# Hybrid decoder layer on one core: the first norm's factor moved into the activations, and four projections fed high and low activations at once

## The chip, the cores and the metric

The kernel runs on one core of a Trainium2 chip. The metric is the device time of one execution in microseconds. TensorE multiplies, VectorE (DVE) and ScalarE (ACT) work elementwise, GpSimd (POOL) too, and SyncE (SP) issues DMAs.

## The reference, cut to what matters

One layer: an RMSNorm of the input, one combined projection whose columns feed three token mixers (HGRN2, Mamba-2, RWKV-7) and the sigmoid gates that merge them, then an output projection, and a squared-ReLU MLP behind a second norm.

```python
u = rmsnorm(h, ln1_w[l])            # x * rsqrt(mean(x*x) + eps) * w
p = u @ w_comb                      # all input projections: q f i g | z xs B C dt | r k v ... | gates
q = silu(q_raw); g = sigmoid(g_raw) # HGRN2
y = y * silu(z)                     # Mamba-2
gates = sigmoid(p_gate)             # 3 branches x 2048
mixed = gates[0]*(o_h @ w_up_h) + gates[1]*(o_m @ w_up_m) + gates[2]*(o_r @ w_up_r)
h = h + mixed @ w_out
u = rmsnorm(h, ln2_w[l])
h = h + square(relu(u @ w_mlp_in)) @ w_mlp_out
out = rmsnorm(h, lnf_w)
```

There are 256 tokens and 16 learned ones before them (272 columns, `T`); the width is 2048, which is 16 blocks of 128 (`KT`).

## The kernel before

Activations lie with channels in the partitions and tokens in the columns. A product makes one tile of 128 output channels: it goes through the 16 blocks of input channels and adds up in one PSUM bank. To keep float32 accuracy every operand is split in a high part, rounded to the type `fp32r`, and a low part, what is left; of the four products of parts three are made. `product` (L229) does that with three matmuls per block: weights high by activations high, weights high by activations low, weights low by activations high. `product2` (L243) does the first two as one matmul of twice the columns (512): the result stands in two halves of the bank, which the caller adds. Before, the output projection and the MLP use `product2`; the input projection and the three branch projections use `product`.

`weights` (L213) loads a tile's weights in pieces of 8 blocks (512 KB, on SP's queue, three raw buffers) and splits each on ScalarE (L201, the cast) and VectorE (L202, the low part); there are three buffers for the high parts and three for the low ones, so about a tile and a half ahead. It runs with high priority.

The input norm (L290 to L367). `x_parts` multiplies x by the norm's weight `ln1` and splits it into `uh` and `ul`, without the norm's factor. The first four column tiles (`FIRST`: wl, aldt and two of gl) run while x and their weights arrive. The squares of x are summed by ScalarE (L359) and GpSimd (L361, L362), a matmul with ones sums over the partitions (L364), and `inv_sqrt` makes the factor `rstd1`, one per token. Since the factor depends on the token alone, it is applied to each result: `proj` (L369) multiplies the PSUM tile by `rstd1` (L371), and L367 does so for the first four. Constants (`omu` to `lbt`, L378 to L397) are worked out behind the last part of x.

After that come the stages of RWKV-7 (`r_stage1`, `r_inverse`, `r_solve`; tiles r, k, v), of Mamba-2 (`m_tile`, `m_gate`; tiles xs, z, B, C), of the gates (`gates_ahead`, written to DRAM until they are needed) and of HGRN2 (`h_cols`, `h_chain`; tiles f, i, q, g), placed among each other by hand; then the branch projections, the output projection, the MLP. PSUM has three banks for such tiles (`trunk_psum`) and five for the rest (`mx`).

The order of instructions on each engine is made by a planner: it plays the program through with estimated times and takes on each engine the instruction of highest priority that is ready; program order is the priority, a `tc.high_priority()` block comes ahead of it, and `tc.issue_after(ins)` sets an instruction behind another one on its engine. On the chip each engine then runs its list in order.

## Time and profile before

| | |
|---|---|
| median of 3 runs | 1914.78 us (1914.56 to 1915.48) |
| the profiled execution | 1914.41 us |
| its span, first to last instruction | 1912.6 us |
| TensorE (PE) busy | 1890.1 us, 99% |
| weight loads (PEld) busy | 1747.1 us, 91% |
| VectorE busy | 1289.5 us, 67% |
| ScalarE busy | 1074.5 us, 56% |
| GpSimd busy | 187.5 us, 10% |
| read from HBM | 327.72 MB (written 10.08 MB; 177 GB/s over the span) |

Busy time of TensorE is modelled: a matmul's row lasts longer than the time until the next one may start, so the time of a stream is read from starts, not from durations. Of a matmul, `pt<-uh,wh` names the output tile and the operands, and `128x256` the partitions and columns of the output. A few matmul records can be missing from a trace.

### The profile page before, as it was taken

The page shows a single profiled execution, that of the slowest core. Times are in us where ns is not written, and L with a number is a line of the kernel's source. Part 1 is how long each engine was busy: PE and PEld are TensorE (multiplying, and loading weights), DVE is VectorE, ACT ScalarE, POOL GpSimd, SP SyncE. Part 2 cuts the span into 40 slices and gives each one's busy share as a digit, 9 for nine tenths or more (in the row PEclk, how much of TensorE's full clock was granted, in tenths as well). Part 3 has the DMA queues.
Part 4 walks back from the last instruction along what each step waited for, and adds up shares of the span by engine and source line. Part 5 has one row for each costly group of instructions (what it writes and reads, how often), then busy time and mean ns, then how long its engine had stood idle before and what let it go on. Part 6 is the DMA issues. An engine that isn't in the chain of part 4 may idle for free.

```text
span 1912.6 us, 35367 instructions
## 1 busy us (share of the span) xinstructions
PE 1890.1 (99%) x13910; PEld 1747.1 (91%) x13910; DVE 1289.5 (67%) x2126; ACT 1074.5 (56%) x1943; POOL 187.5 (10%) x317
## 2 busy tenths in 40 slices
PE   7999999999999999999999999999999999999997
PEld 7999999999999999999999988888888888888886
DVE  7878667567956566777677776654566556675575
ACT  6666566566556667766564455544454345435554
POOL 5110111112111111112111100000000000000000
PEclk9999999999999999999999999999999999999998
DMA  6556544354554445445656765555555555555552
GB/s 241 181 187 198 159 145 154 127 164 157 177 165 155 144 144 194 144 146 169 203 166 212 251 220 193 185 187 188 186 187 187 188 186 187 188 187 188 187 187 100
DMA packets 104103, 340.12 MB, mean 178 GB/s; under 512 B 18216, under 2 KB 21432, under 8 KB 103936
## 3 DMA queue, kind: packets, MB, share of 16 engines
q1 hardware_dynamic: 92480, 316.79, 50.3%
q0 software_dynamic: 8576, 17.67, 3.0%
q10 hardware_dynamic: 2880, 3.39, 0.5%
q8 instruction: 109, 1.79, 0.4%
q14 instruction: 58, 0.48, 0.1%
HBM read 327.72 MB, written 10.08 MB: 177 GB/s over the span
## 4 chain that ended last, share of the span: by engine, by line
PE 98%; DVE 1%; DMA 0%; ACT 0%; issue 0%; SPq 0%; DVEq 0%
PE pt L251 28%; PE pt L239 15%; PE pt L237 15%; PE pt L238 15%; PE pt L253 14%; PE px L1093 1%; PE px L619 1%; DMA xt<-in_xt 0%; PE px L725 0%; PE px L707 0%; PE px L633 0%; PE px L762 0%; PE px L627 0%; PE px L548 0%; PE px L346 0%; PE px L691 0%
## 5 line engine op out<-in xcount | busy, mean ns | idle before, releaser
L202 DVE TENSOR_TENSOR wl<-raw,wh 128x1024 fp32r<-128x1024 f32 (+1 forms) x593 | 726.4, 1225 | 397.3 <-ACT wh L201 389.4
L201 ACT CAST wh<-raw 128x1024 fp32r<-128x1024 f32 (+1 forms) x593 | 621.9, 1049 | 652.8 <-PE pt L238 239.1
L237 PE MATMUL pt<-uh,wh 128*128 128x256 f32 (+2 forms) x1984 | 567.9, 286 | 0.0
L239 PE MATMUL pt<-uh,wl 128*128 128x256 f32 (+3 forms) x1984 | 567.4, 286 | 0.0
L238 PE MATMUL pt<-ul,wh 128*128 128x256 f32 (+2 forms) x1984 | 567.0, 286 | 0.0
L237 PEld LDWEIGHTS pt<-uh,wh 128*128 128x128 f32 x1984 | 374.1, 189 | 3.4 <-issue 1.5
L239 PEld LDWEIGHTS pt<-uh,wl 128*128 128x128 f32 x1984 | 373.9, 189 | 3.4 <-issue 1.9
L238 PEld LDWEIGHTS pt<-ul,wh 128*128 128x128 f32 x1984 | 373.4, 188 | 3.7 <-issue 1.7
L251 PE MATMUL pt<-z,wh 128*128 128x512 f32 x1024 | 362.2, 399 | 0.0
L251 PE MATMUL pt<-hx,wh 128*128 128x512 f32 x1024 | 358.9, 393 | 0.0
L253 PE MATMUL pt<-hx,wl 128*128 128x256 f32 x1024 | 287.9, 283 | 0.0
L253 PE MATMUL pt<-z,wl 128*128 128x256 f32 x1024 | 287.4, 281 | 0.0
L251 PEld LDWEIGHTS pt<-z,wh 128*128 128x128 f32 x1024 | 192.4, 188 | 48.0
L251 PEld LDWEIGHTS pt<-hx,wh 128*128 128x128 f32 x1024 | 191.6, 188 | 43.6
L253 PEld LDWEIGHTS pt<-z,wl 128*128 128x128 f32 x1024 | 193.4, 189 | 0.1
L253 PEld LDWEIGHTS pt<-hx,wl 128*128 128x128 f32 x1024 | 192.5, 188 | 0.9
L239 PE MATMUL pt<-oh,wl 128*128 128x256 f32 x384 | 108.3, 282 | 0.0
L237 PE MATMUL pt<-oh,wh 128*128 128x256 f32 x384 | 108.2, 282 | 0.0
L238 PE MATMUL pt<-ol,wh 128*128 128x256 f32 x384 | 107.3, 279 | 0.0
L371 DVE TENSOR_TENSOR pt<-pt,rstd 128x256 f32<-128x256 f32 (+3 forms) x124 | 54.1, 436 | 56.2 <-PE pt L239 55.7
L251 PE MATMUL pt<-m,wh 128*128 128x512 f32 x256 | 89.8, 393 | 0.0
L1298 POOL TENSOR_TENSOR macc<-h,rs 128x256 f32<-128x256 f32 x3 | 2.1, 720 | 825.9 <-ACT rs L1292 825.9
(459 smaller groups left out, 2218.2 us busy)
## 6 DMA issues: line engine op xcount, KB each, us to landing
raw<-in_w SPq DMA_DIRECT2D x591, 512.0 KB, 3.5
rcb<-sc_rc SPq DMA_DIRECT2D x8, 256.0 KB, 3.7
sc_gr<-gt POOLq DMA_DIRECT2D x16, 128.0 KB, 3.6
sc_gm<-gt POOLq DMA_DIRECT2D x16, 128.0 KB, 3.6
sc_gh<-gt POOLq DMA_DIRECT2D x16, 128.0 KB, 3.6
gin<-sc_gr POOLq DMA_DIRECT2D x16, 128.0 KB, 2.7
gin<-sc_gm POOLq DMA_DIRECT2D x16, 128.0 KB, 2.8
gin<-sc_gh POOLq DMA_DIRECT2D x16, 128.0 KB, 3.3
```

The lines of the kernel that those rows point to most:

```text
L201: act.copy(dst_h, src)
L202: vec.tensor_tensor(dst_l, src, dst_h.bitcast(F32), sub)
L237: pe.matmul(ps, lhsT=wh[:, j], rhs=hi[:, kt, tok], start=(kt == 0), stop=False)
L238: pe.matmul(ps, lhsT=wh[:, j], rhs=lo[:, kt, tok], start=False, stop=False)
L239: pe.matmul(ps, lhsT=wl[:, j], rhs=hi[:, kt, tok], start=False, stop=(k == last and j == 7))
L251: pe.matmul(full.rearrange("p (a n) -> p a n", a=2), lhsT=wh[:, j], rhs=x[:, :, kt], start=(kt == 0), stop=end, skip_group_check=True)
L253: pe.matmul(full[:, :NR], lhsT=wl[:, j], rhs=x[:, 0, kt], start=False, stop=end, skip_group_check=True)
L371: vec.tensor_tensor(ps, ps, rstd1[:, tok], mult)
L619: pe.matmul(pk[e][:, c], lhsT=kt_[er, t], rhs=ar[er, :, t], start=True, stop=True)
L1093: pe.matmul(px[br, 2 * i + c], lhsT=xc, rhs=xc, start=True, stop=True)
L1298: nc.gpsimd.tensor_tensor(macc[:, c], h1[:, c], rf, mult)
```

## The change

The factor moves from the results into the activations. The first four tiles still run on x times `ln1` and get their multiplication afterwards. The rest of the kernel uses other activations: when the factor is there, x is multiplied in place by `ln1` and the factor (16 instructions on VectorE) and split again into `uh` and `ul` (four splits of four blocks each, ScalarE and VectorE), which overwrites what the first four tiles read. `proj` is then only `product`, without a multiplication. The additions of the squares move from GpSimd to VectorE, the last of them becomes a second matmul with ones, and the whole chain gets high priority, except the 16 multiplications. `uh` and `ul` become halves of one tile `u`, so that one access pattern reaches both.

A new helper, `proj2`, makes the tiles of the gates and of z, q and g with `product2` over the 256 real tokens: ScalarE copies the low half out of PSUM, VectorE adds it to the high one. For the gates and g the sum goes to SBUF, for z and q it stays in PSUM. The constants `lbt` of HGRN2 move to the beginning of that stage.

```diff
@@ -283,13 +283,13 @@
     st_u = ExitStack()
     upool = pool(st_u, "upool")
-    uh = upool.tile([P, KT, T], F32R, name="uh")
-    ul = upool.tile([P, KT, T], F32R, name="ul")
-    rstd1 = upool.tile([P, T], F32, name="rstd1")
+    u = upool.tile([P, 2, KT, T], F32R, name="u")
+    uh, ul = u[:, 0], u[:, 1]
     with ExitStack() as st:
         np_ = pool(st, "norm1", side="right")
         xt = np_.tile([P, KT, T], F32, name="xt")
+        rstd1 = np_.tile([P, T], F32, name="rstd1")
         FIRST = (("wl", ALL), ("aldt", ALL), (("gl", 0), REAL2), (("gl", 1), REAL2))
         def raw_piece(key, k, parts=1):
@@ -353,22 +353,34 @@
                     x_parts(4 * i + 4, 4 * i + 8)
         ssum = np_.tile([P, 2, T], F32, name="ssum")
-        for q in range(8):
-            sq = np_.tile([P, 2, T], F32, tag="sq", bufs=2, name=uname("sq"))
-            with tc.issue_after(last_x[0]):
-                act.activation(sq if q else ssum, xt[:, 2 * q:2 * q + 2], AF.Square)
-            if q:
-                nc.gpsimd.tensor_tensor(ssum, ssum, sq, add)
-        nc.gpsimd.tensor_tensor(ssum[:, 0], ssum[:, 0], ssum[:, 1], add)
-        ssq = mx()[:, :T]
-        pe.matmul(ssq, lhsT=C("ones"), rhs=ssum[:, 0], start=True, stop=True)
-        inv_sqrt(rstd1, ssq, 1.0 / D, eps_n)
+        with tc.high_priority():
+            for q in range(8):
+                sq = np_.tile([P, 2, T], F32, tag="sq", bufs=2, name=uname("sq"))
+                with tc.issue_after(last_x[0]):
+                    act.activation(sq if q else ssum, xt[:, 2 * q:2 * q + 2], AF.Square)
+                if q:
+                    with tc.issue_after(last_x[1]):
+                        vec.tensor_tensor(ssum, ssum, sq, add)
+            ssq = mx()[:, :T]
+            for k in range(2):
+                pe.matmul(ssq, lhsT=C("ones"), rhs=ssum[:, k], start=(k == 0), stop=(k == 1))
+            inv_sqrt(rstd1, ssq, 1.0 / D, eps_n)
+        for kt in range(KT):
+            vec.scalar_tensor_tensor(xt[:, kt], xt[:, kt], V("ln1", kt), rstd1, mult, mult)
+        with tc.high_priority():
+            for q in range(4):
+                s = slice(4 * q, 4 * q + 4)
+                split(uh[:, s], ul[:, s], xt[:, s])
         for ps, (_, tok) in zip(first, FIRST):
             vec.tensor_tensor(ps, ps, rstd1[:, tok], mult)
     def proj(key, tok=ALL, ahead=True):
-        ps = product(key, uh, ul, tok, ahead=ahead)
-        vec.tensor_tensor(ps, ps, rstd1[:, tok], mult)
+        return product(key, uh, ul, tok, ahead=ahead)
+
+    def proj2(key, t):
+
+        ps, lo = product2(key, u[:, :, :, NM:])
+        act.copy(t, lo)
         return ps
@@ -384,17 +396,6 @@
     nwa = const.tile([P, 16], F32, name="nwa")
     vec.tensor_scalar(nwa, V("w0", 0, 16), -1.0, None, mult)
     nw0, na0 = nwa[:, 0:8], nwa[:, 8:16]
-
-    lbt = const.tile([P, 6, 8], F32, name="lbt")
-    lg = V("lb", 0, 8)
-    vec.tensor_tensor(lbt[:, 0], lg, lg, ALU.max)
-    vec.tensor_tensor(lbt[:, 1], lg, lbt[:, 0], sub)
-    act.activation(lbt[:, 1], lbt[:, 1], AF.Exp)
-    vec.reciprocal(lbt[:, 2], lbt[:, 1])
-    vec.tensor_tensor(lbt[:, 3], lbt[:, 1], lbt[:, 2], mult)
-    vec.tensor_tensor(lbt[:, 4], lbt[:, 3], lbt[:, 3], sub)
-    vec.tensor_scalar(lbt[:, 5], lbt[:, 4], -1.0, 1.0, mult, add)
-    lb, omlb = lbt[:, 4], lbt[:, 5]
     late.close()
@@ -923,8 +924,9 @@
         vec.scalar_tensor_tensor(o_m[:, t], xs[:, NM:], V("md", t), py[:, :NR], mult, add)
     def m_gate(t):
-        ps = proj(("z", t), REAL)
         s = mt("zs", NR)
+        ps = proj2(("z", t), s)
+        vec.tensor_tensor(ps, ps, s, add)
         sigmoid(s, ps)
         vec.tensor_tensor(s, ps, s, mult)
         vec.tensor_tensor(o_m[:, t], o_m[:, t], s, mult)
@@ -958,9 +960,10 @@
                 return
             key = early[len(sc_g)]
             sc_g[key] = dr.tile([P, NR], F32, name=f"sc_{key[0]}{key[1]}")
-            ps = proj(key, REAL)
             t = wp.tile([P, NR], F32, tag="gt", bufs=2, name=uname("gt"))
-            sigmoid(t, ps)
+            ps = proj2(key, t)
+            vec.tensor_tensor(t, ps, t, add)
+            sigmoid(t, t)
             nc.gpsimd.dma_start(sc_g[key], t)
     m_open()
@@ -1013,6 +1016,18 @@
     def ht(tag, shape, bufs=1):
         return hp.tile([P, *shape], F32, tag=tag, bufs=bufs, name=uname(tag))
+
+    lbt = const.tile([P, 6, 8], F32, name="lbt")
+    lg = V("lb", 0, 8)
+    vec.tensor_tensor(lbt[:, 0], lg, lg, ALU.max)
+    vec.tensor_tensor(lbt[:, 1], lg, lbt[:, 0], sub)
+    act.activation(lbt[:, 1], lbt[:, 1], AF.Exp)
+    vec.reciprocal(lbt[:, 2], lbt[:, 1])
+    vec.tensor_tensor(lbt[:, 3], lbt[:, 1], lbt[:, 2], mult)
+    vec.tensor_tensor(lbt[:, 4], lbt[:, 3], lbt[:, 3], sub)
+    vec.tensor_scalar(lbt[:, 5], lbt[:, 4], -1.0, 1.0, mult, add)
+    lb, omlb = lbt[:, 4], lbt[:, 5]
+
     NH = 2
     itm_ = [zeroed(f"itm{n}", [NH, P], hp) for n in range(2)]
@@ -1045,12 +1060,14 @@
                 pe.transpose(ptr[:hi - lo, 128 * n:128 * n + 128], iv[:, lo:hi], ident)
             act.copy(it[:, i], ptr[:, :256].rearrange("p (a b) -> p a b", a=2))
             act.copy(itm[:NM, i], ptr[:NM, 256:384])
-            ps = proj(("q", h), REAL)
             sq = ht("sf", (T,), 2)
+            ps = proj2(("q", h), sq[:, :NR])
+            vec.tensor_tensor(ps, ps, sq[:, :NR], add)
             sigmoid(sq[:, :NR], ps)
             vec.tensor_tensor(q[:, i], ps, sq[:, :NR], mult)
-            ps = proj(("g", h), REAL)
-            sigmoid(sg[:, i], ps)
+            ps = proj2(("g", h), sg[:, i])
+            vec.tensor_tensor(sg[:, i], ps, sg[:, i], add)
+            sigmoid(sg[:, i], sg[:, i])
     def h_chain(hb):
         pfx, k, q, sg, it = hs.pop(hb)
```

## Rows read from the trace of the kernel before

**Rows 1.** The page: busy times, and the granted clock in 40 slices of the span.

```profile
PE 1890.1 (99%) x13910; PEld 1747.1 (91%) x13910; DVE 1289.5 (67%) x2126; ACT 1074.5 (56%) x1943; POOL 187.5 (10%) x317
...
PEclk9999999999999999999999999999999999999998
```

**Rows 2.** The waits of TensorE: waiter, releaser, us in total, times, longest.

```profile
PE px L346 <- ACT wh L201: 8.4, 2, 6.2
PE px L1285 <- ACT sqe L1284: 1.9, 1, 1.9
```

**Rows 3.** Busy time by stretch: us from:to, length, engines (instructions), clock, DMA.

```profile
480.00:540.00 60.00, 60.00 (x506) 58.96 (x505) 52.81 (x106) 35.88 (x62) 10.70 (x16) 1.00 0.61 196
...
1200.00:1880.00 680.00, 680.00 (x3863) 592.69 (x3863) 418.10 (x584) 323.46 (x477) 0.00 (x0) 1.00 0.57 187
```

**Rows 4.** Timeline of TensorE, ends of long stretches: start, us, line, operands, [idle].

```profile
491.35 0.39 PE L237 MATMUL pt<-uh,wh 128*128 128x256 f32 x1
...
528.61 0.28 PE L239 MATMUL pt<-uh,wl 128*128 128x256 f32 x1
...
1267.66 0.39 PE L251 MATMUL pt<-hx,wh 128*128 128x512 f32 x1
...
1357.54 0.40 PE L251 MATMUL pt<-z,wh 128*128 128x512 f32 x1
...
1447.99 0.39 PE L251 MATMUL pt<-hx,wh 128*128 128x512 f32 x1
```

**Rows 5.** Timeline of TensorE, 272 columns: seven starts, the first and the last.

```profile
49.33 0.29 PE L238 MATMUL pt<-ul,wh 128*128 128x272 f32 x1
...
50.09 0.28 PE L238 MATMUL pt<-ul,wh 128*128 128x272 f32 x1
```

**Rows 6.** Groups by line and shape: count | busy us, mean ns | idle before.

```profile
L371 DVE TENSOR_TENSOR pt<-pt,rstd 128x256 f32<-128x256 f32 x72 | 31.1, 431 | 37.8 <-PE pt L239 37.5
L1255 DVE TENSOR_TENSOR pt<-pt,lo 128x256 f32<-128x256 f32 x64 | 27.2, 426 | 0.0
...
L1221 ACT COPY lo<-pt 128x256 f32<-128x256 f32 x80 | 29.3, 366 | 3.9 <-PE pt L253 3.9
```

**Rows 7.** Timeline of TensorE around its wait, and where the first four tiles end.

```profile
20.27 0.28 PE L348 MATMUL px<-ul,wh 128*128 128x258 f32 x1
22.78 0.40 PE L346 MATMUL px<-uh,wh 128*128 128x272 f32 x1 [2.23 <-ACT wh L201]
...
37.33 0.62 PE L364 MATMUL px<-ssum,ones 128*128 128x272 f32 x2
37.58 0.48 PE L237 MATMUL pt<-uh,wh 128*128 128x258 f32 x1
```

**Rows 8.** Timeline of ScalarE.

```profile
21.59 0.21 ACT L392 ACTIVATE lbt<-lbt 128x8 f32<-128x8 f32 x1 [1.59 <-DVE lbt L391]
...
38.36 0.48 ACT L265 ACTIVATE rstd<-px,eps 128x272 f32<-128x272 f32 x1
```

**Rows 9.** Timeline of VectorE and GpSimd ("x8": merged, us of all).

```profile
15.07 3.49 DVE L325 SCALAR_TENSOR_TENSOR ul<-xt,vecs,uh 128x272 fp32r<-128x272 f32 x8
...
18.73 0.16 DVE L383 TENSOR_SCALAR nkk<-vecs 128x8 f32<-128x8 f32 x1
18.76 2.77 POOL L361 TENSOR_TENSOR ssum<-ssum,sq 128x544 f32<-128x544 f32 x2
...
20.26 1.30 DVE L391 TENSOR_TENSOR lbt<-vecs,lbt 128x8 f32<-128x8 f32 x1
```

**Rows 10.** Groups by line and shape, VectorE and ScalarE.

```profile
L202 DVE TENSOR_TENSOR wl<-raw,wh 128x1024 fp32r<-128x1024 f32 x591 | 725.1, 1227 | 396.9 <-ACT wh L201 389.0 <-ACT gt L677 0.5
...
L201 ACT CAST wh<-raw 128x1024 fp32r<-128x1024 f32 x591 | 620.8, 1051 | 652.8 <-PE pt L238 239.1 <-PE pt L251 237.6 <-issue 162.6
```

**Rows 11.** Timeline of TensorE in the first tiles.

```profile
13.53 0.43 PE L348 MATMUL px<-ul,wh 128*128 128x272 f32 x1
13.76 0.43 PE L350 MATMUL px<-uh,wl 128*128 128x272 f32 x1
```

## The prediction

> **What bounds the kernel now.** I read the page's busy times and its slices first: TensorE is busy for 99% of the span, and its granted clock stands at nine tenths or more up to the last slice [rows 1]. So a saving elsewhere counts only where TensorE waits. The view of its waits names where: 8.4 us in two waits for weight casts, both within the first 23 us, and 1.9 us just before the output [rows 2]. For some 1,850 us between them it waits for nothing; there the price of an edit is what it adds to or takes from the stream of matmuls. That leaves two places: the stream, and the stretch in which the first four column tiles end and the next begin.
>
> The third view is the load of weights. The weight-load row is busy 98% of the time where a step takes three matmuls, and 87% where `product2` takes two [rows 3]. That looks like a second bound which the change relieves; the time of a step decides it. In the timeline, 315 records in a row of `product` over `uh`, `ul` (256 columns each) start from 491.35 to 528.61 us: 37.26 us over 314 intervals, 118.7 ns each, 356.0 ns for a step of three. `product2` takes 256 steps from 1267.66 to 1357.54 us, 351.1 ns each, and 256 from there to 1447.99 us, 353.3 ns each [rows 4]. Both forms stream 768 columns per step, and one load in three fewer changes it by 1%. The 272-column matmuls start 0.127 us apart (0.76 us over six) [rows 5], against 0.119 for 256: the interval grows with the columns, which a bound by loads would not do. Columns are the bound.
>
> **The change part by part.** All sums are made against the profiled execution, 1914.41 us, of which the span is 1912.6; the median of the runs is 1914.78, 0.02% above it.
>
> (1) High and low activations in one matmul: 48 gate tiles and 8 each of z, q and g make 72 tiles (the 72 multiplications of their shape in [rows 6]), 16 steps each, 1,152 steps. A step goes from 355 to 356 ns (the 356.0 holds one late return from small matmuls) to 351.1 or 353.3 [rows 4]: 1.8 to 4.9 ns less, 2.1 to 5.6 us in all. I take 355.5 to 352.2, so -3.8 us. What no row shows is `product2` on these strides; if it is as slow as three matmuls the term is 0, and I let it reach +1.
>
> (2) What follows a tile of those 72: VectorE's multiplication by the factor (431 ns) becomes an addition of the low product (426 ns in the MLP), and ScalarE gets a copy of 366 ns, 72 x 0.366 = 26 us over the kernel [rows 6]. The multiplications of the other tiles go without a replacement. I cost all this at nothing: the cover is three PSUM buffers, with 16 x 0.352 = 5.6 us of TensorE work per tile, against 0.8 us more before a buffer is free. TensorE waits for neither engine there [rows 2]. Were the cover gone, each of the 72 tiles could cost up to 0.8 us. The seven small operations of `lbt` in the HGRN stage cost nothing there either, under the same cover; their price is at the place they leave.
>
> (3) The place they leave. TensorE stands from 20.27 to 22.78 us and then waits for a weight cast [rows 7]. ScalarE, which runs in order, had the exponential of `lbt` before that cast, at 21.59 us, after 1.6 us of waiting for VectorE's L391 [rows 8]. L391 takes 1.30 us for 8 columns where L383 takes 0.16 for as many, and it lies inside GpSimd's two additions of L361, 18.76 to 21.53 us [rows 9]. The change removes the exponential from there and the GpSimd additions too: up to 2.2 us of TensorE's time. [...]
>
> (4) What comes in. Until now the tile `r` starts as soon as the first four are done: the product with ones stands at 37.33, `r` at 37.58 us [rows 7]. Now `r` needs `uh`, `ul` multiplied by the factor, and the factor needs all of x. VectorE's work between its last part of x (15.07 + 3.49 = 18.56 us [rows 9]) and the last low part of `u`:
> - seven additions of 544 elements: 0.44 us for 272 (next line) and 1.227 for 1,024 [rows 10] give 0.73 each between them, 5.1 us;
> - 16 multiplications of 272: the eight of L325 take 3.49 us [rows 9], 0.44 each, 7.0 us;
> - four low parts of 1,088: the same 1.227 us gives 1.30 each, 5.2 us;
> - low parts of weights that TensorE also needs: five left of the first four tiles' eight, two of `r`, one of `k`, 8 x 1.227 = 9.8 us.
>
> Together 27.1 us: 45.7 us if VectorE never stands. Between the last addition and the factor lie two products with ones (0.25 us each, one more than now: +0.3 us of TensorE with its hand-over), the logarithm (0.48 us [rows 8]) and an exponential of that size, 1.5 us in which VectorE can do one weight part; with hand-overs the last low part ends at about 47 us. ScalarE has less to do there: squares, casts and copies, none of the additions and multiplications. Before, `r` and `k` end at about 37.58 + 48 x 0.120 + 48 x 0.127 = 49.4 us. After, if the planner puts the first half of `k` (24 matmuls, 3.0 us) into the gap, there remain at 47 us a quarter of `r` (1.45 us) and half of `k` (3.0 us): 51.5 us, +2.1. If nothing fills the gap: 47 + 1.45 + 6.1 = 54.5 us, +5.1. The saving of (3) is in this already: an earlier end of the first four tiles gives nothing while VectorE sets the end. I take the middle, +3.6, since three weight buffers allow about half a tile ahead. Ends: -2.2 us, if VectorE's chain is hidden and only (3) is left; +11.0, below. Queued behind the new waits: on ScalarE the weight casts, behind squares that wait for VectorE's additions (two `sq` buffers); on SP the weight loads, each of which needs a raw buffer that a low part frees; on GpSimd the memsets of tiles that take the place of `xt`, not needed until later stages.
>
> Sum: 1914.41 - 3.8 + 0.3 + 3.6 = 1914.5 us.
>
> **The rivals.** *Serial factor* (slower). The planner leaves the products with ones behind the first four tiles, where the one is now, 37.33 us [rows 7], or VectorE's additions come so late that it is the same. Then 0.5 us of products, 1.0 of logarithm and exponential, 1.8 of four multiplications, 1.1 for a copy of 1,088 elements (a cast of 1,024 takes 1.05 [rows 10]), 1.3 for a low part and some 0.3 of hand-overs: `r` starts at 43.3 us, +5.7. Each of its three later quarters needs 4 x 0.44 + 1.3 us of VectorE, and with a weight part for every 2.9 us of matmuls some 4.2 us, against 1.45 us of matmuls: another 8.3 us, of which `k` fills 3.0; in all +11.0. That is 1914.41 - 3.8 + 0.3 + 11.0 = 1921.9 us. [...] Against it: the diff puts the chain ahead in priority, and behind the gap of 2.5 us the pace was not lower: the 120 matmuls left of the first four tiles take 14.55 us, 0.121 each [rows 7]. It decides once the factor comes later than about 34 us.
>
> *Chain hidden* (faster). The planner sets the factor early and fills the gap with `k`; (3) gives its 2.2 us, the stream the full 5.6: 1914.41 - 2.2 + 0.3 - 5.6 = 1906.9 us, or 1908.7 with my stream. Against it stands VectorE's sum, 27 us of work in a stretch of 19.
>
> *Loads were the bound* (faster by far). 1,152 loads fewer, at the interval of 118.7 ns, would be 137 us: 1778 us. The stretches of [rows 4] speak against it, and so does the interval of [rows 5]. [...]
>
> *It doesn't do what it says*: `product2` on the halves of `u` is no better than three matmuls, 0 to +1 in place of -3.8: 1918.3 to 1919.3 us, the edge of no change; it is in the range and in the slower chance.
>
> **How the numbers follow.** A difference under 0.2%, 3.8 us, can't be told from none, so no change is 1911.0 to 1918.6 us. The forecast, 1914.5 with a range of its own from 1911 to 1918.6, has a chance of 0.62: two terms of opposite sign that nearly cancel, each uncertain by some 2 us. Serial factor, with the strided case, 0.22; chain hidden 0.14; loads 0.02. So faster 0.16, same 0.62, slower 0.22. The range for eight in ten goes from 1909.0, just above the hidden case, to 1923.0, past the serial case without the clock.
>
> **What would show it.** In the trace after: a step of the gates of 351 to 354 ns for (1). Of TensorE's waits, the one near 20 us gone or shorter for (3), and for (4) a new one of 2 to 6 us between the first four tiles and `r`, put down to VectorE's low part (L202), with `k`'s tile ending near 52 us. No wait of TensorE between 60 and 1,890 us for (2). Wrong would be: new waits in the middle, which would mean that the planner's new order, not the operations, sets the time; or a gate's step far from 351 to 356 ns.

## The result, and the profile after

The changed kernel takes 1926.13 us (median of 4 runs, 1924.3 to 1927.52) against 1914.67 (4 runs): a ratio of 1.0058, 95% interval 1.0045 to 1.0072. It is slower by 11.5 us, outside the range of the prediction. Its profiled execution takes 1926.36 us, the span 1924.6.

The page after, busy times and granted clock, to lay beside [rows 1]:

```profile
PE 1894.0 (98%) x12760; PEld 1696.0 (88%) x12760; DVE 1278.1 (66%) x2101; ACT 1096.2 (57%) x2019; POOL 173.7 (9%) x309
...
PEclk9999999999999999999999999999999999999999
```

1,150 matmul records fewer, and TensorE is busy for longer. The waits of TensorE, to lay beside [rows 2]:

```profile
PE px L346 <- ACT wh L201: 6.2, 1, 6.2
PE pt L238 <- DVE u L202: 4.9, 1, 4.9
PE pt L251 <- DVE zs L931: 2.1, 2, 1.7
PE pt L251 <- ACT k L259: 2.0, 1, 2.0
...
PE pt L237 <- ACT wh L201: 0.9, 1, 0.9
...
PE pt L237 <- DVE zs L931: 0.2, 1, 0.2
```

Before, TensorE waited for nothing between the first tiles and the output. Now there is a wait of 4.9 us for the low part of `u`, one of 0.9 us for a weight cast just before it, and 4.3 us of waits in the middle (`zs`, `k`). The waits are not the whole price. Busy times by stretch of the kernel after, columns as in [rows 3] (the number before the DMA share is the granted clock):

```profile
40.00:45.00 5.00, 1.92 (x9) 1.92 (x10) 5.00 (x8) 1.73 (x3) 0.00 (x0) 0.68 0.34 107
45.00:50.00 5.00, 5.00 (x29) 5.00 (x29) 4.55 (x7) 1.43 (x4) 0.00 (x0) 0.63 0.32 108
50.00:55.00 5.00, 5.00 (x43) 5.00 (x42) 2.51 (x5) 4.88 (x10) 0.00 (x0) 1.00 0.20 52
...
745.00:750.00 5.00, 2.98 (x12) 2.29 (x12) 3.93 (x9) 4.75 (x11) 0.00 (x0) 0.84 0.37 116
750.00:755.00 5.00, 5.00 (x27) 4.31 (x27) 5.00 (x10) 4.57 (x12) 4.49 (x11) 0.82 0.09 25
```

Two stands of TensorE (times in which it waits and does nothing), of 4.9 and 2.0 us, go with a stretch at a lower granted clock: in slices of 1 us it is 0.50 from 42 to 48 and from 749 to 751 us, and 1.00 again from 49 and from 752 us. 29 matmuls start from 45 to 50 us, 43 in the next five. A stretch of 5 us at a mean clock c lacks (1 - c) x 5 us of full pace: 1.60 + 1.85 at the front, 0.80 + 0.90 near 750 us, 5.15 us in all. At the front part of that falls into the stand itself, where no work was to be done; what the matmuls lost there is read from their starts below. Outside these rows no stretch of 5 us between 25 and 1,900 us is below 1.00, and in the profiled execution of before none is.

Where the 12 us that the span grew by arise is read from two landmarks that both kernels have: the first small product of RWKV's fourth `r_stage1`, and the first matmul of the output projection. TensorE's timeline before, then after:

```profile
115.73 0.39 PE L500 MATMUL px<-twl,lora 96*128 96x272 f32 x1
...
1086.94 0.40 PE L251 MATMUL pt<-m,wh 128*128 128x512 f32 x1
```

```profile
123.39 0.39 PE L501 MATMUL px<-twl,lora 96*128 96x272 f32 x1
...
1098.89 0.39 PE L251 MATMUL pt<-m,wh 128*128 128x512 f32 x1
```

After is 7.66 us behind at the first and 11.95 at the second; from there to the end both take 825.7 us. So two thirds are lost at the front, and 4.3 us between the landmarks, in spite of the stream's gain.

**The front.** VectorE's timeline after, and ScalarE's first copy of `u`:

```profile
32.97 6.69 DVE L369 SCALAR_TENSOR_TENSOR xt<-xt,vecs,rstd 128x272 f32<-128x272 f32 x16 [0.61 <-ACT rstd L266]
39.58 0.44 DVE L375 TENSOR_TENSOR px<-px,rstd 128x272 f32<-128x272 f32 x1
39.93 1.21 DVE L202 TENSOR_TENSOR wl<-raw,wh 128x1024 fp32r<-128x1024 f32 x1
41.06 0.77 DVE L375 TENSOR_TENSOR px<-px,rstd 128x272 f32<-128x272 f32 x2
41.75 1.28 DVE L202 TENSOR_TENSOR u<-xt,u 128x1088 fp32r<-128x1088 f32 x1
...
34.81 1.10 ACT L201 CAST u<-xt 128x1088 fp32r<-128x1088 f32 x1
```

The factor is there early, at 32.9 us. But all 16 multiplications come in one run, then three of the first tiles' own multiplications and a weight part, and only at 41.75 us the first low part of `u`, although the four blocks it reads were multiplied after the first four and ScalarE's high part of them was done at 35.9 us. TensorE's timeline after:

```profile
37.83 0.39 PE L237 MATMUL pt<-u,wh 128*128 128x272 f32 x1 [0.90 <-ACT wh L201]
43.08 0.58 PE L238 MATMUL pt<-u,wh 128*128 128x258 f32 x1 [4.86 <-DVE u L202]
43.46 0.42 PE L239 MATMUL pt<-u,wl 128*128 128x258 f32 x1
43.68 0.42 PE L237 MATMUL pt<-u,wh 128*128 128x258 f32 x1
...
57.08 0.29 PE L239 MATMUL pt<-u,wl 128*128 128x272 f32 x1
```

It stands for 4.9 us and then starts matmuls 0.22 us apart (near 13.6 us before, 0.23 for 272 columns [rows 11]), in place of 0.12: the 23 intervals from 43.46 to 48.55 us take 5.09 us, where 0.119 us each for 258 columns (the 14 intervals from 48.73 to 50.40 us) and 0.127 for 272 [rows 5] would make 2.8. So the lower pace costs about 2.3 us here. The last matmul of `r` and `k` starts at 57.08 us; before it was 49.46.

**The stream** does what the change says. A stretch of 74 steps without another matmul between, after, the first and the last L251:

```profile
509.35 0.50 PE L251 MATMUL pt<-u,wh 128*128 128x512 f32 x1
...
534.95 0.40 PE L251 MATMUL pt<-u,wh 128*128 128x512 f32 x1
```

25.60 us over 73 intervals are 350.7 ns for a step of two matmuls, against the 356.0 of [rows 4] for a step of three.

**The branch products** (`oh`, `ol`; 24 tiles, 1,152 matmuls) are not touched by the change, and are slower. 530 records before, then 506 after:

```profile
1024.52 0.28 PE L238 MATMUL pt<-ol,wh 128*128 128x256 f32 x1
...
1086.82 0.28 PE L239 MATMUL pt<-oh,wl 128*128 128x256 f32 x1
```

```profile
1038.18 0.28 PE L238 MATMUL pt<-ol,wh 128*128 128x256 f32 x1
...
1098.77 0.28 PE L239 MATMUL pt<-oh,wl 128*128 128x256 f32 x1
```

That is 117.8 ns per matmul before and 120.0 after, 2.5 us over 1,152.

**The middle.** The tile of z in the first wait for `zs`, ScalarE's copy of its low half and VectorE's last reading of the high one; TensorE behind two of the waits; and, from the kernel before, VectorE's first and last use of the second tile of z:

```profile
464.58 0.37 ACT L383 COPY zs<-pt 128x256 f32<-128x256 f32 x1
...
472.66 0.41 DVE L931 TENSOR_TENSOR zs<-pt,zs 128x256 f32<-128x256 f32 x1
...
492.44 0.51 PE L251 MATMUL pt<-u,wh 128*128 128x512 f32 x1 [1.67 <-DVE zs L931]
...
747.72 0.50 PE L251 MATMUL pt<-u,wh 128*128 128x512 f32 x1 [2.00 <-ACT k L259]
```

```profile
461.43 0.43 DVE L371 TENSOR_TENSOR pt<-pt,rstd 128x256 f32<-128x256 f32 x1
...
468.44 0.41 DVE L929 TENSOR_TENSOR zs<-pt,zs 128x256 f32<-128x256 f32 x1
```

The sum of z goes back to PSUM, and the tile is held through the sigmoid for 8.5 us. That is not new: before, this tile of z was held through the sigmoid for 7.4 us, and TensorE did not wait. By the two traces what differs is what TensorE runs meanwhile. Before, 38 of the 58 matmuls in those 7.4 us belong to column tiles, 4.9 us of work; after, in the 8.5 us, 45 of 46 do, 8.4 us of work, so that TensorE comes to need the held buffer.

### The profile page after: what moved, and what is told of

It is laid out like the page before. It is cut to its first block, busy times and chain, and to the rows that moved or that the text cites. A ratio compares the mean times of both kernels' runs of the same rounds, so it can differ in the third digit from the quotient of the medians.

```text
span 1924.6 us, 33164 instructions
## 1 busy us (share of the span) xinstructions
PE 1894.0 (98%) x12760; PEld 1696.0 (88%) x12760; DVE 1278.1 (66%) x2101; ACT 1096.2 (57%) x2019; POOL 173.7 (9%) x309
## 4 chain that ended last, share of the span: by engine, by line
PE 97%; DVE 1%; ACT 0%; DMA 0%; issue 0%; SPq 0%; DVEq 0%; ACTq 0%
PE pt L251 42%; PE pt L253 22%; PE pt L237 8%; PE pt L239 8%; PE pt L238 8%; PE px L1110 1%; PE px L620 1%; PE px L726 0%; PE px L708 0%; PE px L634 0%; DMA xt<-in_xt 0%; PE px L763 0%; PE px L628 0%; DVE xt L369 0%; PE px L917 0%
## 5 line engine op out<-in xcount | busy, mean ns | idle before, releaser
L251 PE MATMUL pt<-u,wh 128*128 128x512 f32 x1152 | 412.9, 397 | 4.1 <-DVE zs L931 2.1
L251 PE MATMUL pt<-z,wh 128*128 128x512 f32 x1024 | 362.2, 399 | 0.0
L251 PE MATMUL pt<-hx,wh 128*128 128x512 f32 x1024 | 358.9, 393 | 0.0
L253 PE MATMUL pt<-u,wl 128*128 128x256 f32 x1152 | 328.9, 285 | 0.0
L251 PEld LDWEIGHTS pt<-u,wh 128*128 128x128 f32 x1152 | 217.2, 189 | 52.8 <-DVE zs L931 2.6
L238 PE MATMUL pt<-u,wh 128*128 128x272 f32 (+2 forms) x832 | 242.1, 291 | 4.9 <-DVE u L202 4.9
L237 PE MATMUL pt<-u,wh 128*128 128x272 f32 (+2 forms) x832 | 243.1, 292 | 1.1 <-ACT wh L201 0.9
L239 PE MATMUL pt<-u,wl 128*128 128x272 f32 (+2 forms) x832 | 242.1, 291 | 0.0
L251 PEld LDWEIGHTS pt<-z,wh 128*128 128x128 f32 x1024 | 192.4, 188 | 47.9
L251 PEld LDWEIGHTS pt<-hx,wh 128*128 128x128 f32 x1024 | 191.6, 188 | 43.6
L253 PEld LDWEIGHTS pt<-u,wl 128*128 128x128 f32 x1152 | 217.2, 189 | 3.8 <-issue 1.9
L238 PEld LDWEIGHTS pt<-u,wh 128*128 128x128 f32 x832 | 157.9, 190 | 6.0 <-DVE u L202 5.1
L237 PEld LDWEIGHTS pt<-u,wh 128*128 128x128 f32 x832 | 157.8, 190 | 3.4 <-ACT wh L201 1.1
L239 PEld LDWEIGHTS pt<-u,wl 128*128 128x128 f32 x832 | 157.7, 190 | 1.3 <-issue 0.5
```

The source lines that it names most:

```text
L237: pe.matmul(ps, lhsT=wh[:, j], rhs=hi[:, kt, tok], start=(kt == 0), stop=False)
L238: pe.matmul(ps, lhsT=wh[:, j], rhs=lo[:, kt, tok], start=False, stop=False)
L239: pe.matmul(ps, lhsT=wl[:, j], rhs=hi[:, kt, tok], start=False, stop=(k == last and j == 7))
L251: pe.matmul(full.rearrange("p (a n) -> p a n", a=2), lhsT=wh[:, j], rhs=x[:, :, kt], start=(kt == 0), stop=end, skip_group_check=True)
L253: pe.matmul(full[:, :NR], lhsT=wl[:, j], rhs=x[:, 0, kt], start=False, stop=end, skip_group_check=True)
```

## The experiments

Four theories: **A**, the order on VectorE at the front (with the lower pace behind TensorE's stand) is the main loss. **B**, the branch products are slower because `rstd1`, 1,088 bytes per partition, left the pool in front of everything allocated later, so that their operands lie at other addresses. **C**, the loss lies in the paired tiles (those of `proj2`) and what follows them. **D**, the planner uses up the shorter column tiles too early, and too little is left to stand between the dependent small matmuls of the RWKV chain.

| kernel | median us (range, runs) | ratio to before, 95% |
|---|---|---|
| `norm_only` | 1924.54 (1924.04 to 1924.7, 4) | 1.0049 [1.0034, 1.0064] |
| `quarters` | 1920.35 (1918.72 to 1923.65, 6) | 1.0029 [1.0017, 1.0041] |
| `pad` | 1924.19 (1923.62 to 1924.74, 4) | 1.0047 [1.003, 1.0063] |
| `quarters_pad` | 1918.24 (1916.64 to 1919.78, 11) | 1.0018 [1.001, 1.0027] |
| `norm_quarters` | 1917.03 (1916.53 to 1917.52, 11) | 1.0013 [1.0004, 1.0022] |
| `lbt` | 1911.99 (1911.42 to 1912.61, 10) | 0.9987 [0.9978, 0.9996] |
| `pair_only` | 1920.36 (1918.48 to 1921.77, 8) | 1.0028 [1.0018, 1.0039] |
| `lbt_qg` | 1912.88 (1912.25 to 1913.88, 11) | 0.9990 [0.9981, 0.9999] |
| `zfree` | 1930.83 (1929.42 to 1931.23, 5) | 1.0078 [1.0065, 1.0091] |
| `after_all_nt` | 1922.37 (1921.69 to 1926.04, 5) | 1.0038 [1.0026, 1.0051] |
| `pair_tie` | 1945.14 (1944.94 to 1945.36, 4) | 1.0158 [1.0141, 1.0175] |
| `after_tie` | 1953.41 (1952.95 to 1953.96, 4) | 1.0201 [1.0186, 1.0217] |
| `sum_lbt_pair_tie` | 1942.8 (1942.17 to 1943.7, 4) | 1.0146 [1.0131, 1.0161] |
| `pair_tie6` | 1932.09 (1930.75 to 1934.68, 4) | 1.0088 [1.0074, 1.0102] |
| `pair_tie7` | 1925.4 (1924.22 to 1927.67, 5) | 1.0056 [1.0042, 1.007] |
| `lbt_pair_tie7` | 1924.61 (1922.86 to 1926.49, 5) | 1.0052 [1.004, 1.0065] |

The kernel before took 1914.5 to 1914.8 beside each of them.

### The front: `norm_only`, `quarters`, `norm_quarters`

`norm_only` is the kernel after with three matmuls in all tiles again (the other three places likewise):

```diff
-            ps = proj2(key, t)
-            vec.tensor_tensor(t, ps, t, add)
-            sigmoid(t, t)
+            ps = proj(key, REAL)
+            sigmoid(t, ps)
```

> The factor in the activations, but three matmuls per step in all tiles as before the change. Theory A (the loss is made where the first four tiles end: VectorE does all 16 multiplications ahead of the first low part, TensorE stands 5 to 6 us and then runs slowly): the tile k ends near 57 us again, no long wait of TensorE between 60 and 1890 us, and with the branch products still 120 ns apart (theory B, below) 1923 to 1927 us. Theory C (the loss is made in the middle, by what follows the 72 tiles): 1914 to 1917 us.

1924.54, 9.8 us more than before without a single paired tile: C falls as the main cause. The same wait of 4.9 us stands behind the first tiles, the clock rows give 0.54 and 0.78 from 40 to 50 us, the branch products take 120.0 ns, and there is no wait in the middle.

`quarters` changes the order on VectorE alone:

```diff
+        lows = []
+        with tc.high_priority():
+            for q in range(4):
...
+                with tc.issue_after(lows[q - 2]) if q > 1 else ExitStack():
+                    for kt in range(4 * q, 4 * q + 4):
+                        vec.scalar_tensor_tensor(xt[:, kt], ..., rstd1, mult, mult)
+                act.copy(uh[:, s], xt[:, s])
+                lows.append(vec.tensor_tensor(ul[:, s], ..., sub).ins)
+        with tc.issue_after(lows[3]):
             for ps, (_, tok) in zip(first, FIRST):
                 vec.tensor_tensor(ps, ps, rstd1[:, tok], mult)
```

> The changed kernel with VectorE's order mended: the multiplications of blocks 8 to 11 come behind the low part of blocks 0 to 3, those of 12 to 15 behind the low part of 4 to 7, and the multiplications of the first four tiles behind the last low part. Theory A: the first low part ends near 39 us instead of 43, the wait of TensorE falls from 4.9 to about 2 us and the pace stays high: 1920 to 1923 us. Rival (VectorE's sum of work is what counts, in whatever order): k ends near 57 us and the time stays at 1925 to 1927 us.

1920.35, 5.8 us less than after, as A says. VectorE, then TensorE, then a stretch of `quarters`:

```profile
33.15 3.39 DVE L374 SCALAR_TENSOR_TENSOR xt<-xt,vecs,rstd 128x272 f32<-128x272 f32 x8 [0.42 <-ACT rstd L266]
...
37.59 1.29 DVE L376 TENSOR_TENSOR u<-xt,u 128x1088 fp32r<-128x1088 f32 x1
```

```profile
38.94 0.38 PE L238 MATMUL pt<-u,wh 128*128 128x258 f32 x1 [0.54 <-DVE u L376]
```

```profile
40.00:45.00 5.00, 4.03 (x33) 3.81 (x32) 5.00 (x9) 1.50 (x2) 0.00 (x0) 1.00 0.40 123
```

The first low part starts 4.2 us earlier, the wait of 4.9 is 0.5 (with one of 1.0 us for a weight part behind it), and the clock stays at 1.00 in this execution up to the output. The landmark of the fourth `r_stage1` comes at 117.92 us: 2.2 behind before in place of 7.66. The executions of this kernel differ: a span of 1917.3 us at a mean clock of 0.998, 1921.8 at 0.995. So the same lists of instructions spend more or less time at a lower clock. The traced execution of `quarters_pad` (next section), which has the same order, shows it at the front, around stands of 0.9, 0.6 and 0.6 us:

```profile
40.00:45.00 5.00, 4.44 (x20) 4.13 (x20) 5.00 (x8) 1.10 (x1) 0.00 (x0) 0.50 0.35 104
```

Its landmark comes at 119.75 us, 4.0 behind before. In both traces the mended order takes the long stand away, but the lower pace is not tied to that stand and comes back in one of them.

`norm_quarters` is `norm_only` with both that order and the bytes of the next section:

> norm_only (the factor in the activations, three matmuls in every tile) with VectorE's order by quarters and the 1,088 bytes of pad. Of norm_only's 9.5 us up to the first product with m, 7.1 stand at the front, 2.5 in the branch products. In quarters the front's share was 2.2. So the factor's new place with both mended should be worth 2.2 us against before: 1916.9 (1916 to 1918). If it comes out at 1914 to 1915, the 72 multiplications taken off VectorE were worth what the front costs; at 1919 to 1921, the front's loss is one of norm_only's own.

1917.03 (expected 1916.9), with the landmark at 117.68 us and no stretch below 1.00 between 25 and 1,900 us. So the factor's new place, in the best order tried, still costs 2.3 us. The move of `lbt` is in this kernel too; beside `lbt` alone (below, 1911.99) it costs 5.0.

### The address: `pad`, `quarters_pad`

```diff
     uh, ul = u[:, 0], u[:, 1]
+    pad_u = upool.tile([P, T], F32, name="pad_u")
+    nc.gpsimd.memset(pad_u[:, :1], 0.0)
```

> The changed kernel with 1,088 unused bytes per partition behind u, where the factor lay before the change, so that the tiles allocated after it lie where they lay before. Theory B (the interval of matmuls depends on where the operands lie): the branch products go back from 120.0 to 117.8 ns apart, 1,152 matmuls, so about 2.5 us less, 1923 to 1924 us. Rival (it comes from what else runs then): 120 ns and 1926 us stay.

> quarters with the 1,088 bytes a partition of pad. If the mended order and the mended address are apart, 1920.4 less 1.9 to 2.5: 1918.2 (1917.5 to 1919). If the half pace behind the waits in the middle comes back, as it did in the kernel with the sums in SBUF, up to 3.4 us more: 1920 to 1922.

506 branch products of `pad`:

```profile
1037.67 0.28 PE L238 MATMUL pt<-ol,wh 128*128 128x256 f32 x1
...
1097.15 0.28 PE L239 MATMUL pt<-oh,wl 128*128 128x256 f32 x1
```

59.48 us over 505 intervals, 117.8 ns: nothing but the place of what is allocated behind `u` differs from after (and one small memset on GpSimd), so B holds. The other traces agree: the five kernels without those 1,088 bytes behind `u` read 120.0 ns in their longest run of branch products, the 13 with them 117.8. `pad` gains 1.9 us on after, `quarters_pad` 2.1 on `quarters`. Which operand it is, and what about its address matters, was not tried.

### The wait near 20 us: `lbt`

The kernel before, with the block of `lbt` moved to the beginning of the HGRN stage, as in the change, and nothing else.

> The kernel before with the constants lbt moved to the HGRN stage, nothing else. If the wait of 2.2 us near 20 us is the exponential's, it goes and the time is 1912 to 1913.5 us; if the cast waits for something else (its weights, a buffer), 1914 to 1915.5 us.

1911.99, 2.6 us less than before and the fastest kernel here. TensorE's timeline where [rows 7] has the wait of 2.23 us:

```profile
19.84 0.28 PE L348 MATMUL px<-ul,wh 128*128 128x258 f32 x1
20.15 0.39 PE L346 MATMUL px<-uh,wh 128*128 128x272 f32 x1
```

GpSimd's additions stay in this kernel. VectorE and GpSimd there:

```profile
19.26 5.82 DVE L202 TENSOR_TENSOR wl<-raw,wh 128x1024 fp32r<-128x1024 f32 x3
...
17.95 6.05 POOL L361 TENSOR_TENSOR ssum<-ssum,sq 128x544 f32<-128x544 f32 x3
```

Three weight parts take 1.94 us each beside them, against a mean of 1.227 over the 591 of before [rows 10]; why is not shown. It costs TensorE nothing here, since it waits for no weight part: what made it wait was the exponential in front of ScalarE's cast.

### The paired tiles: `pair_only`, `lbt_qg`, `zfree`, `after_all_nt`

`pair_only` is the kernel before with `product2` in the 72 tiles and the factor multiplied behind it. Unlike the change it puts the sums of z and q into SBUF, and each of the 72 tiles has one more VectorE operation:

```diff
+    def proj2(key, t):
+        ps, lo = product2(key, u[:, :, :, NM:])
+        act.copy(t, lo)
+        vec.tensor_tensor(t, ps, t, add)
+        vec.tensor_tensor(t, t, rstd1[:, REAL], mult)
...
-            ps = proj(key, REAL)
             t = wp.tile([P, NR], F32, tag="gt", bufs=2, name=uname("gt"))
-            sigmoid(t, ps)
+            proj2(key, t)
+            sigmoid(t, t)
```

> The kernel before with the 72 tiles on product2 alone; the factor is multiplied into the sum in SBUF (one more VectorE operation for each of the 72). Theory A: no wait where the first four tiles end beyond the 2.2 us of before, the steps 351 ns instead of 355 to 356, TensorE's stream 5 to 8 us shorter: 1906 to 1911 us. Theory C: the longer tail of each tile makes new waits in the middle, 1914 us or more.

1920.36, some 10 us above theory A's figure and in the range of C. To see where, each interval between two starts on TensorE, from one landmark to the other, is put to the first of the two; waits over 0.15 us are taken out and summed apart. The 72 tiles: 422.0 us before, 414.4 here, -7.6; that is the stream's gain. The small matmuls of the chains: 162.8 before, 170.0 here, +7.2. The waits: none before, 4.3 here. All other tiles: +1.1. (Its front is 0.7 us ahead of before.) Three of the waits, and the stretch behind them:

```profile
PE px L947 <- POOL nsq L943: 2.6, 1, 2.6
...
PE px L726 <- DVE yy L724: 0.9, 1, 0.9
PE px L753 <- DVE rq L746: 0.6, 1, 0.6
```

```profile
740.00:745.00 5.00, 3.30 (x10) 2.79 (x11) 3.10 (x8) 4.40 (x13) 4.12 (x10) 0.66 0.00 0
```

All three end between 731 and 742 us, where the chain ends without column tiles between its steps. The 1.7 us that the clock lacks in that stretch fall mostly on column tiles that start behind the last wait. The 7.2 us of the small matmuls are spread over the chain. The planner's order did change: when the chain reaches its 57th matmul of L707, in its eighth and last iteration, column tiles worth 501 us (their columns at 0.46 ns each, from 356.0 ns for the 768 of a step) are done before, at 686 us; here 547, at 729 us. But this is not the loss of the changed kernel, where the same sum over the small matmuls gives 163.9 us, only 1.1 more than before.

`lbt_qg` is `lbt` with the paired matmul in the 16 tiles of q and g alone, behind the RWKV chain:

> The kernel lbt with the paired matmul in the 16 tiles of q and g alone (256 of the 1,152 steps), which stand behind the RWKV chain; z and the 48 gate tiles keep three matmuls, the factor stays on VectorE behind each sum. If the paired step is worth what the 72 tiles showed (6.7 us for 1,152 steps, 5.8 ns each) and nothing of it is lost where no RWKV chain runs beside it, 1.5 us are won: 1910.5 (1910 to 1911). If the loss to slower small matmuls comes with the paired step anywhere, in its share (11.2 us for 1,152 steps), 1912.5 to 1914.

1912.88: no gain over `lbt` (1911.99). By the same sums the 72 tiles take 1.4 us less, the small matmuls 1.3 more and the other tiles 0.8 more.

`zfree` is the kernel after with the sums of z and q in SBUF:

```diff
-        s = mt("zs", NR)
-        ps = proj2(("z", t), s)
-        vec.tensor_tensor(ps, ps, s, add)
+        zv_ = mt("zv", NR)
+        ps = proj2(("z", t), zv_)
+        vec.tensor_tensor(zv_, ps, zv_, add)
...
```

> The kernel after, with the sums of z and of q written into SBUF (zv, and q's own rows) and not back into the PSUM tile, so that a PSUM tile is free once ScalarE has copied one half and VectorE has added the other; it is no longer held through the sigmoid and the multiplication. Nothing else is changed. Theory 'held PSUM': TensorE's waits put to VectorE zs (2.1 us, twice, and 0.2) go, the span falls by 2 to 2.3 us: 1923 to 1924.5. Rival 'order only': TensorE wants the next operands as late as before, the waits appear under another name (weights' halves or a chain's matmul) and the time stays at 1926 (1925 to 1927). The wait put to k at 745 us (2.0 us) is untouched by either.

1930.83, 4.7 us slower than after. The waits for `zs` are gone, but others have come:

```profile
PE px L943 <- POOL nsq L939: 2.3, 1, 2.3
...
PE px L917 <- DVE xd L892: 1.0, 1, 1.0
```

With the wait for `k` (1.1 us here) they sum to as much as before the edit, and the clock from 745 to 755 us is 0.66, 3.4 us short in place of 1.7. The held PSUM tile made the wait for `zs`, but without it the small matmuls take 167.3 us in place of 163.9. The same split runs through all kernels that pair the 72 tiles without holding gate tiles back: 167 to 170 us where the sums of z and q go to SBUF (`pair_only`, `zfree`, `after_all_nt`), 164 where they stay in PSUM (after, `pad`, `quarters`, `quarters_pad`). Why is not shown.

`after_all_nt` is after with the edits of `quarters`, `pad` and `zfree` together (z's sum in a buffer that was there already):

> The kernel after with three edits together, each of which undoes one suspected loss: VectorE's multiplications by quarters as in quarters, the 1,088 bytes a partition as in pad, and z's and q's sums in SBUF as in zfree. If the three losses are apart from each other, their parts add: 1926.1 less 5.8, less 1.9, less 2.2 gives 1916.2 (1915 to 1917.5), still above the kernel before, and what is left over against before is the slower small matmuls of the RWKV chain that pair_only showed. Rival 'one critical path in the middle': what is won at the front is lost where the chain makes TensorE wait, 1919 to 1921.

1922.37. The parts don't add: it has the `nsq` and `xd` waits of `zfree` (1.8, 1.0 us), its small matmuls take 167.3 us as in `zfree`, and the clock is short by 5.1 us (from 35 to 45 and 740 to 750 us), though its waits at the front are as short as those of `quarters`.

### Holding gate tiles back: `pair_tie` to `lbt_pair_tie7`

If D is right, gate tiles held back should fill the end of the chain again. `pair_tie` is `pair_only` with:

```diff
         for i in range(4):
             for m, n in zip(odd, even):
-                pe.matmul(pg[m, i], ...)
+                mm = pe.matmul(pg[m, i], ...)
+                solves.setdefault(p, mm.ins)
...
-        gates_ahead(AHEAD[4])
+        with tc.issue_after(solves[p]):
+            gates_ahead(AHEAD[4])
```

> pair_only with one thing more: the six gate tiles placed behind each of the last four r_solve steps may not start on TensorE before that step's first matmul. Theory D (product2 makes the planner put 34 to 47 us more of trunk products ahead of the RWKV chain, so that at the chain's end no trunk product is left to cover its waits): the trunk products done by the eighth py matmul fall from 547 us to near the 500 us of before, the small matmuls go from 180 back to some 170 us, and the time to 1906 to 1911 us. Rival (the longer tail of each tile costs it, wherever it lies): 1918 us or more stay.

> The changed kernel with the same tie alone. Theory D: the 2.0 us wait for L259 and the 2 us before the norm's matmul near 745 us go, and some of the waits of the z tiles; 1920 to 1924 us, with the 7.7 us at the first tiles still in. Rival: 1926 us stay, or more, because held-back tiles leave TensorE waiting earlier.

> The factor stays on the results; taken over from the change are product2 for the 72 tiles, the sums of squares on VectorE with priority and the moved lbt, with the tie. By theories A and D: 1914.7 - 7 (stream) - 1 (wait near 20 us) + 0.3 (second product with ones) = 1905 to 1909 us, faster than both kernels. If theory D is wrong: 1916 us or more.

`after_tie` is the kernel after with the same tie, `sum_lbt_pair_tie` is `pair_tie` with the move of `lbt` and the sums of squares on VectorE. All three come out 29 us or more above what was expected: they hold back the very tiles that filled the second `r_inverse`, and TensorE stands there for 27.5 us in `pair_tie` (22.1 and 29.0 in the others). So the tie was put on p = 6 and 7 only, and then on p = 7:

> pair_only with the six gate tiles behind iterations p = 6 and 7 alone held behind that iteration's first solve; those of p = 4 and 5 stay free, so that the second inverse keeps the tiles that filled it (what pair_tie took away). Theory 'run-ahead': the small matmuls after 720 us are slower in pair_only (waits of 2.6, 0.9 and 0.6 us and about 5 us spread) because the 72 tiles are used up too early and too little trunk work is left to stand between the chain's dependent matmuls; held back, they come back: the waits of 2.6, 0.9 and 0.6 go, the span falls by 4 to 8 us, 1912 to 1916. Rival 'shorter cover': the chain's matmuls are slower because each tile that stands between two of them is shorter, wherever it is put; the time stays within 2 us of pair_only, 1918.5 to 1922, or rises if the tie delays the tiles' own outputs.

> pair_only with the six gate tiles of the last iteration alone (p = 7) held behind that iteration's first solve. Theory 'run-ahead': these 34 us of trunk work then stand beside the last solve and the second group's norm, where pair_only waits 2.6, 0.9 and 0.6 us and falls to half pace (1.7 us); those go and some of the 5 us spread over the chain's matmuls, 1912 to 1917. Rival 'shorter cover': within 2 us of pair_only, 1918.5 to 1922. If these six tiles were themselves the filler of p = 6, new stands of TensorE appear there and the time rises above 1922, as in pair_tie6.

> The same with the lower bounds' table moved as in lbt. The two edits touch different stretches (20 us, and 640 to 750 us), so it should be pair_tie7 less 2.7 us; under 'run-ahead' 1909 to 1914, and under 'shorter cover' 1916 to 1919.

All three are slower than `pair_only` (1932.09, 1925.4 and 1924.61), and the move of `lbt` gains 0.8 us on `pair_tie7` where 2.7 were expected. Each time the held tiles were missed one step earlier. `pair_tie7`, a wait and a stretch:

```profile
PE px L639 <- ACT set_42vz L619: 3.3, 1, 3.3
```

```profile
680.00:685.00 5.00, 4.94 (x22) 3.85 (x22) 1.27 (x3) 1.44 (x5) 0.00 (x0) 0.50 0.01 3
```

From 660 to 690 us the clock is short by 10.2 us, part of it while TensorE stands. These runs show how much the chain needs the tiles; they don't show that a better order of them gives the 7.2 us back. D is neither shown nor refuted.

## Why the prediction was wrong

Each term of the forecast beside what the landmarks and the sums between them give (the kernel after, profiled executions):

| | forecast us | found us |
|---|---|---|
| front, up to the fourth `r_stage1` | +3.9 | +7.7 |
| matmuls of the 72 tiles | -3.8 | -4.8 |
| waits in the middle (`zs` 2.3, `k` 2.0) | 0 | +4.3 |
| small matmuls of the chains | 0 | +1.1 |
| branch products | 0 | +2.8 |
| all other tiles | 0 | +0.9 |
| sum | +0.1 | +12.0 |

The -4.8 holds the stretch at a clock of 0.84 and 0.82 near 750 us, 1.7 us by the clock rows, which falls on these tiles: without it the stream gained some 6.5 us. The step, 355.5 to 350.7 ns, gives 5.5 for 1,152.

- **What bounds the kernel**, and (1): right. Columns set the step; with a third of the loads gone it fell by 1.5%, and *Loads were the bound* and *It doesn't do what it says* are refuted. The term was somewhat too small.
- **(2)** failed: it put at nothing what came to +4.3 us of waits. The cover of three PSUM buffers was counted with 0.8 us more before a buffer is free; the sigmoid for which z's tile stays in PSUM, 8.5 us here, was not in it, and the absence of waits before was taken as room. And no step of the text asked what the planner does with shorter column tiles: they now stand in a row where small matmuls stood between them. The text named "new waits in the middle" as what would prove it wrong, and gave it no price. `pair_only` and `lbt_qg` show besides that, with the sums in SBUF, the small matmuls take back nearly all that the stream gives.
- **(3)** right, and shown alone by `lbt`: -2.6 us where up to 2.2 was predicted. In the changed kernel the gain is covered, as the text said, since VectorE sets the end there.
- **(4)** failed, and is the largest part: +7.7 us at the front in place of +3.9. The step that failed is the one from VectorE's sum to the end of `r`. The sum was good: the last low part was put at 47 us and stands at 48.1. But TensorE waits for the first quarter's low part, and that was taken to follow its four multiplications. In the trace the 16 multiplications stand in one run, 6.69 us, and the first low part ends at 43.0. Why the planner listed them so is not shown. *Serial factor* had the wrong mechanism: it let the case decide by a factor later than 34 us, and the factor was there at 32.9. That its start of `r`, 43.3 us, is close to the 43.08 of the first matmul behind the stand is chance. The forecast has no term for a lower clock, and its range ends at the serial case without one; the trace of after shows a clock of 0.68 and 0.63 from 40 to 50 us, about 2.3 us by the starts. `quarters` returns 5.5 of the 7.7 us in an execution without the lower pace at the front; the 2.2 left are near the forecast's lower case, +2.1 and 0.3 for the second product with ones.
- **Not in the text at all**: the branch products. `rstd1` moves to another pool, and the text gives that no price.

What stays open: the 7.2 us spread over the chain in `pair_only`; why the planner put the 16 multiplications first; why a lower clock (0.84 and 0.82) follows a stand of 2.0 us near 747 us in the kernel after and none a stand of 1.98 us at the same place in `quarters`; which operand's place costs the 2 ns.

## What to carry to other kernels

Where an engine's list is made ahead, cost a new chain by the time of the first result that the bound engine (here TensorE) needs, and read from the diff in which order its parts can be listed; a sum that ends on time says nothing of the first part. A stand of the bound engine can have a second price at a lower clock, here from nothing behind 1.98 us in `quarters` to 1.7 us, by the clock rows, behind 2.0 us in after, so a short wait in a stream without any can cost more than its length. Faster filler need not be a gain where a chain of dependent steps has to be filled: measure the part alone, as `lbt` was, and keep what holds (here that is the small move of `lbt`, 0.13%).

## What was not expected of the hardware

- The start-to-start time of 256-column matmuls on unchanged code (the branch products) was 117.8 ns in the kernel before and in `pad`, which have 1,088 bytes per partition in front of what is allocated behind `u`, and 120.0 in the kernel after, which has not.
- After a stand of 4.9 us TensorE's matmuls started 0.22 us apart and the granted clock was 0.68 and 0.63 in two stretches of 5 us; a clock of 0.66 to 0.84 followed stands of 2.0 to 2.6 us near 745 us in after, `zfree` and `pair_only`, and one of 0.50 was granted around the three short stands at the front of `quarters_pad`. The stand of 2.2 us near 20 us in the kernel before had no such stretch. The stands ended with VectorE (4.9 us, `u` in after), ScalarE (2.0 us, `k` in after) and GpSimd (2.3 us in `zfree`, 2.6 in `pair_only`, both `nsq`).
